# Expert places of 64, 96, 64, 96, 96, 64, 96, 64 slots with the first expert in one of 64, and the norm's weight row moved from routing to the gathered rows

## The chip, the core and the metric

The kernel runs on one core of a Trainium2 chip. The metric is the device time of one execution in microseconds, the median of the runs. Of the core's engines the text speaks of TensorE (PE, matrix products; its weight loads are PEld), VectorE (DVE), ScalarE (ACT), GpSimd (POOL) and SyncE (SP), which here does little but issue the transfers that bring weights from HBM. Everything is in float32.

## The reference

A two-layer decoder trunk over 256 tokens of width 1024. Layer 0 has two kinds of attention and a dense SwiGLU, layer 1 a sliding-window attention beside a short convolution and then a top-2-of-8 expert SwiGLU, which is where the change lies:

```python
def moe_swiglu(x, w_router, w_gate, w_up, w_down):      # x = rms_norm(h, norm_ffn)
    xt = x.reshape(B * S, D)                            # 256 x 1024
    logits = (xt @ w_router).astype(jnp.float32)        # 256 x 8
    top_vals, top_idx = lax.top_k(logits, TOP_K)        # 2 of 8
    top_w = jax.nn.softmax(top_vals, axis=-1)
    gates = jnp.einsum('nk,nke->ne', top_w, jax.nn.one_hot(top_idx, N_EXPERTS, ...))
    for e in range(N_EXPERTS):
        y = y + gates[:, e:e + 1] * swiglu(xt, w_gate[e], w_up[e], w_down[e])
def rms_norm(x, g):
    return x * rsqrt(mean(x * x) + eps) * g
```

`swiglu(x) = (silu(x @ w_gate) * (x @ w_up)) @ w_down` with an inner width of 3584, so one expert has 3 x 1024 x 3584 float32 weights, 44 MB, and the eight have 352 MB.

## The kernel before

**The stages.** Layer 0 and the attention of layer 1 run to about 490 us. Then the router chooses (`route1` to `route3`, `logits`, `choose`), and from about 506 us the eight experts run one after the other (`experts`, `L1085`) to the end.

**Places and slots.** An expert works on a fixed number of slots, not on all 256 tokens. `CAPS` (`L32`) gives eight places of 96 or 64 slots. Place 0 always holds expert 0, whose weights can so be loaded before the routing is known; the other seven experts are sorted by how many tokens chose them, and `RANKS` (`L33`) says which of them stands in place 1, 2, ... (rank 0 has most tokens). The weights' addresses of places 1 to 7 are read from `most` into SP's registers (`read_counts`). Should an expert have more tokens than its place has slots, a branch behind everything (`L1317`) runs a further pass for it (`rest`) with that expert's weights loaded again.

**Gather.** `dispatch` makes a 0/1 matrix of tokens by slots on DVE, `gather` multiplies it with the normalised rows `xg` on PE, so that a place's tokens stand side by side, and DVE and ACT copy the product from PSUM to `g`. Places are gathered in groups, `((0,), (1, 2), (3, 4), (5, 6), (7,))`: the first before any expert runs, each other one between the steps of the expert ahead of it.

**Steps and weights.** An expert has 12 steps, each on one transfer of 3584 KB (3.67 MB): two of `gate`, two of `up`, for each half `r` of the inner width, and four of `down`. `into` (`L1140`, matmuls at `L1150`) does a gate or up step: 4 x 4 matmuls for each 32 slots, so 32 for a place of 64 and 48 for one of 96. `down` (`L1186`) does 28 matmuls of 512 columns into `y` (`L1193`), and for a place of 96 another 28 of 256 columns into `yo` (`L1197`). `weights.send()` at the end of each step issues the next transfer of a list into a ring of five buffers `big`, so a transfer's issue on SP (`L1124` for gate and up, `L1132` for down) waits until the step five transfers ahead of it has let its buffer go. Between the steps `put` sets the small work (`fill`): transposes of the hidden rows (`act_T`), the gather of the next group, and the weighted sum of the previous expert's result into `h` (`part_y`, `scatter`).

**The start of the ring.** Two of the five buffers exist since layer 0 and are filled there with expert 0's two first gate transfers. The pool of the other three is opened in `experts_open` (`L1019`) where `np`, `xp` and `parts` lay before; the three transfers that it sends at once (up, up, gate) wait until the last readers of that memory are done. `parts` holds the split weights of the dense layers, three pairs of tiles in one pool.

**Routing.** `route2` (`L898`) squares `h` on ACT for the norm and multiplies `h` by the norm's weight row `gain` on DVE into `xf`; `route3` (`L902`) makes the reciprocal root on POOL and scales `xf` by it into `xg` on ACT. The row itself is a transfer that POOL issues in `route_open`. `final_gain` (`L1280`) is another one, of the weights of the very last norm, into one of the tiles `t.dr`. The router itself works on `h` with the weight row folded into its own matrix (`conv_w`, `L809`).

Of the kernel before, what the change touches and what calls it, by code (L numbers as in the profile page):

```python
# [18 lines left out]
D = 1024  # L19
KD = D // 128  # L20
S = 256
NB = 2
# [6 lines left out]
BIG = 7168  # L29
NPARTS = 3  # L30

CAPS = (96, 64, 96, 64, 96, 64, 96, 64)  # L32
RANKS = (3, 0, 4, 1, 5, 2, 6)  # L33

# [54 lines left out]
def trunk(ctx: ExitStack, tc: tile.TileContext, a: dict, out: bass.AP):  # L89
# [14 lines left out]
    raw_pools = []  # L104
    partss = ExitStack()
    parts = rpool(partss, "parts", NPARTS)
    pre = ExitStack()
    xp = rpool(pre, "xp")
    prec = ExitStack()
    pc_ = rpool(prec, "prec")  # L110
# [40 lines left out]
    def split(u):  # L151
        if u.load.view is None:
            load(u.load)
        v, n, w = u.load.view[:, u.j0:u.j0 + u.n], u.n, u.load.at[4]
        pool, size = parts, 2048
        hi, lo = (pool.tile([128, size], F32R, name=x)[:, :n * w].rearrange("p (k w) -> p k w", k=n)
                  for x in ("whi", "wlo"))
        A.activation(hi, v, AF.Copy)  # L158
        m = w - w // u.pool // 2 * 2 if w >= 256 else w
        V.tensor_tensor(lo[:, :, :m], v[:, :, :m], hi[:, :, :m].bitcast(F32), op=OP.subtract)  # L160
        if m < w:
            G.tensor_tensor(lo[:, :, m:], v[:, :, m:], hi[:, :, m:].bitcast(F32), op=OP.subtract)  # L162
        u.hl = (hi, lo)

    ahead_max = [0]

# [94 lines left out]
    def load_gain(name, eng):  # L261
        t.gain = row(a[name], D, "gain", t.np, eng)
# [54 lines left out]
    place = consts.tile([128, 2, NE], F32, name="place")  # L317
    wr = consts.tile([128, KD, NE], F32, name="wr")
    cs = pc_.tile([128, 2, NB, 48], F32, name="cs")

# [483 lines left out]
    def conv_w():  # L804
# [3 lines left out]
        T.transpose(pcw[:, 1, 0:8], t.g8, ident[:8, :8])  # L808
        V.tensor_tensor(wr, wr, pcw[:, 1, 0:8][:, :, None].to_broadcast([128, KD, NE]), op=OP.mult)  # L809

# [58 lines left out]
    def route_open():  # L869
# [6 lines left out]
        t.hT, t.ww, t.sq = {}, wide(), bank()  # L876
        open_("np", "rt")
        t.xf = t.np.tile([128, NB, D], F32, name="xf")
        load_gain('l1_norm_ffn', G)

# [3 lines left out]
    def route1(b, i):  # L884
        xfT = t.np.tile([128, 4, 128], F32, name="xfT", bufs=2)
        p = tbank()
# [11 lines left out]
    def route2(b, i):  # L898
        A.activation(t.sq, h[:, b, half[i]], AF.Square, scale=1.0 / math.sqrt(D), accum_out=t.rs[:, b, i:i + 1])
        V.tensor_tensor(t.xf[:, b, half[i]], h[:, b, half[i]], t.gain[:, half[i]], op=OP.mult)  # L900

    def route3(b):  # L902
        r = t.rs[:, b]
        V.tensor_scalar(r[:, 2:3], r[:, 0:1], r[:, 1:2], EPS, op0=OP.add, op1=OP.add)
        G.tensor_tensor(r[:, 3:4], r[:, 2:3], nhalf, op=OP.pow)
        A.activation(t.xg[:, b], t.xf[:, b], AF.Copy, scale=r[:, 3:4])

# [111 lines left out]
    def experts_open():  # L1019
        close("np")  # L1020
        pre.close()
        partss.close()
        pws.close()
# [7 lines left out]
        for _ in range(3):  # L1031
            weights.send()
        t.dr = [draw[0].tile([128, RAW], F32, name="raw") for _ in range(2)]
        t.ep = rpool(ctx, "ep", 2)
# [50 lines left out]
    def experts(base, caps, groups, first=(), then=(), finish=()):  # L1085
# [11 lines left out]
        def gather(g, k0):  # L1097
# [6 lines left out]
            for s in g:  # L1104
                if s not in gath:
                    gath[s] = t.ep.tile([128, KD, NG * O], F32, name="g", bufs=3)
                o, v = gath[s][:, k0:k0 + 2, :caps[s]], p[:, :, group[s][1]:group[s][1] + caps[s]]
                if k0 // 2 % 2:
                    V.tensor_copy(o, v)  # L1109
                else:  # L1110
                    A.activation(o, v, AF.Copy)

# [183 lines left out]
    def final3(b):  # L1296
# [4 lines left out]
    finish = [do(final_in)] + [do(final2, b) for b in range(NB)] + [do(final3, b) for b in range(NB)]  # L1301
    mine = experts((0,) * NE, CAPS, ((0,), (1, 2), (3, 4), (5, 6), (7,)), [do(experts_open)],
                   [do(order.close), do(in_order, 'PE'), do(arrange), do(gates), do(read_counts)], finish)
# [52 lines left out]
```

## Time and profile before

| | us |
|---|---|
| median of 3 runs | 1349.49 (1349.46 to 1352.29) |
| the profiled execution | 1352.92 |
| its span, first to last instruction | 1351.1 |
| PE busy | 1287.5 (95%) |
| DVE, ACT, POOL busy | 377.6 (28%), 297.6 (22%), 167.7 (12%) |
| moved by DMA | 432 MB, 320 GB/s over the span |

The page gives each engine's busy time, then the span in 40 equal slices of 33.8 us with busy tenths, then the chain of work that ended last. PE's 95% says little by itself: it is a mean over layers, where the weights are split by three engines, and experts, where PE multiplies what the DMA brings. The chain of the page goes to 76% over PE and to 15% over DMA, nearly all of that on the experts' weights.

### The profile page before, as it was taken

To read this page: it belongs to the slowest core of one execution; us is meant where nothing else is said; L and a number is where in the kernel's file an instruction comes from. 1 tells how busy PE (TensorE), PEld (TensorE's weight loads), DVE (VectorE), ACT (ScalarE), POOL (GpSimd) and SP (SyncE) were. 2 spreads that over 40 slices of the span, in tenths; PEclk is the share of its full clock that TensorE was granted. 3 is DMA by queue.
4 is the path that set the end of the run, shared out by engine and by line. 5 is a ranking of instruction groups with operands and counts; after the bars stand their busy time and mean duration, and the time that the engine had idled before them with its cause. 6 is when DMAs were issued, how large, how long until landed. Compare 5 with 4: busy or idle time off the path is not lost.

```text
span 1351.1 us, 23865 instructions
## 1 busy us (share of the span) xinstructions
PE 1287.5 (95%) x10713; PEld 696.8 (52%) x10713; DVE 377.6 (28%) x704; ACT 297.6 (22%) x471; POOL 167.7 (12%) x117
## 2 busy tenths in 40 slices
PE   7999899999999999999999999989999989999985
PEld 6876678888879773433332343322343323343332
DVE  7666444455465840001100100100100200101202
ACT  6555444333344620101000101001000001000001
POOL 3311344344434110000000000000000000000000
PEclk9998899999999999999999999999999999999997
DMA  8620784555555369989999999999999999999992
GB/s 269 204 93 1 276 297 164 195 176 185 186 168 176 114 244 378 371 342 421 420 429 412 425 430 411 424 426 416 424 426 413 426 421 419 425 419 420 425 421 105
DMA packets 75903, 432.24 MB, mean 320 GB/s; under 512 B 3692, under 2 KB 7808, under 8 KB 71568
## 3 DMA queue, kind: packets, MB, share of 16 engines
q1 hardware_dynamic: 75088, 428.48, 79.6%
q8 instruction: 86, 1.41, 0.4%
q0 software_dynamic: 560, 1.62, 0.4%
q10 hardware_dynamic: 144, 0.52, 0.1%
q14 instruction: 25, 0.20, 0.0%
HBM read 429.57 MB, written 1.05 MB: 319 GB/s over the span
## 4 chain that ended last, share of the span: by engine, by line
PE 76%; DMA 15%; DVE 2%; ACT 1%; POOL 1%; issue 0%; SPq 0%; POOLq 0%; ACTq 0%
PE mm L1150 30%; DMA big<-in_l_w_up_dram 12%; PE y L1193 9%; PE mm L199 8%; PE mm L200 8%; PE mm L201 7%; PE yo L1197 4%; DMA big<-in_l_w_down_dram 2%; PE tt L1102 2%; PE ww L370 1%; PE tt L1177 1%; PE ww L199 1%; PE ww L200 1%; PE ww L201 1%; DMA raw<-in_l_w_gate_dram 1%; PE mm L413 1%
## 5 line engine op out<-in xcount | busy, mean ns | idle before, releaser
L1150 PE MATMUL mm<-big,g 128*32 128x448 f32 x5120 | 497.5, 546 | 20.6 <-DMA big<-in_l_w_up_dram 14.3
L1150 PEld LDWEIGHTS mm<-big,g 128*32 128x32 f32 x5120 | 165.8, 111 | 330.9 <-issue 308.3
L1193 PE MATMUL y<-big,ehT 128*32 128x512 f32 x1792 | 214.7, 593 | 0.5 <-DMA big<-in_l_w_down_dram 0.5
L162 POOL TENSOR_TENSOR wlo<-raw,whi 128x288 fp32r<-128x288 f32 (+6 forms) x74 | 154.5, 2088 | 287.2 <-ACT whi L158 267.0
L160 DVE TENSOR_TENSOR wlo<-raw,whi 128x1760 fp32r<-128x1760 f32 (+6 forms) x74 | 142.9, 1932 | 134.3 <-ACT whi L158 133.9
L158 ACT ACTIVATE whi<-raw 128x2048 fp32r<-128x2048 f32 (+4 forms) x74 | 134.5, 1817 | 154.5 <-PE mm L201 75.2
L199 PE MATMUL mm<-whi,xh 128*128 128x512 f32 (+3 forms) x352 | 138.3, 393 | 1.9 <-ACT whi L158 1.1
L200 PE MATMUL mm<-wlo,xh 128*128 128x512 f32 (+3 forms) x352 | 136.7, 388 | 3.0 <-POOL wlo L162 3.0
L201 PE MATMUL mm<-whi,xl 128*128 128x512 f32 (+3 forms) x352 | 136.7, 389 | 2.4 <-DVE xl L288 2.4
L1178 ACT ACTIVATE ehT<-tt 128x512 f32<-128x512 f32 (+1 forms) x32 | 15.6, 487 | 474.5 <-PE tt L1177 474.4
L1294 POOL TENSOR_TENSOR fs<-fs,nhalf 128x1 f32<-128x1 f32 x2 | 1.1, 548 | 844.1 <-DVE fs L1293 844.1
L1193 PEld LDWEIGHTS y<-big,ehT 128*32 128x32 f32 x1792 | 57.1, 110 | 84.0 <-issue 63.7
L1164 DVE TENSOR_TENSOR hid<-hid,mm 128x448 f32<-128x448 f32 x40 | 24.9, 622 | 264.9 <-PE mm L1150 261.8
L199 PEld LDWEIGHTS mm<-whi,xh 128*128 128x128 f32 x352 | 67.3, 191 | 17.5 <-ACT xh L287 1.7
L201 PEld LDWEIGHTS mm<-whi,xl 128*128 128x128 f32 x352 | 67.2, 191 | 17.6 <-DVE xl L288 4.1
L200 PEld LDWEIGHTS mm<-wlo,xh 128*128 128x128 f32 x352 | 67.3, 191 | 16.9 <-POOL wlo L162 3.3
L1197 PE MATMUL yo<-big,ehT 128*32 128x256 f32 x896 | 68.9, 379 | 0.0
L1197 PEld LDWEIGHTS yo<-big,ehT 128*32 128x32 f32 x896 | 29.1, 110 | 67.0 <-issue 66.6
L1109 DVE COPY g<-tt 128x192 f32<-128x192 f32 (+1 forms) x16 | 4.6, 321 | 162.0 <-PE tt L1102 162.0
L199 PE MATMUL mm<-xh,whi 128*128 128x256 f32 x160 | 46.5, 291 | 0.0
L200 PE MATMUL mm<-xl,whi 128*128 128x256 f32 x160 | 45.3, 283 | 0.0
L201 PE MATMUL mm<-xh,wlo 128*128 128x256 f32 x160 | 45.2, 283 | 0.0
(311 smaller groups left out, 1051.9 us busy)
## 6 DMA issues: line engine op xcount, KB each, us to landing
big<-in_l_w_up_dram SPq DMA_DIRECT2D x32, 3584.0 KB, 26.6
big<-in_l_w_down_dram SPq DMA_DIRECT2D x31, 3584.0 KB, 24.7
big<-in_l_w_gate_dram SPq DMA_DIRECT2D x30, 3584.0 KB, 25.7
raw<-in_l_w_in_dram SPq DMA_DIRECT2D x15, 1024.0 KB, 5.1
raw<-in_l_w_gate_dram SPq DMA_DIRECT2D x14, 1024.0 KB, 5.2
raw<-in_l_w_up_dram SPq DMA_DIRECT2D x14, 1024.0 KB, 5.2
raw<-in_l_w_down_dram SPq DMA_DIRECT2D x14, 1024.0 KB, 5.0
raw<-in_l_w_out_dram SPq DMA_DIRECT2D x8, 1024.0 KB, 5.2
```

Of the source, the lines that this page charges most:

```text
L158: A.activation(hi, v, AF.Copy)
L160: V.tensor_tensor(lo[:, :, :m], v[:, :, :m], hi[:, :, :m].bitcast(F32), op=OP.subtract)
L162: G.tensor_tensor(lo[:, :, m:], v[:, :, m:], hi[:, :, m:].bitcast(F32), op=OP.subtract)
L199: T.matmul(ps, l[0], r[0], start=first, stop=False, **kw)
L200: T.matmul(ps, l[0], r[1], start=False, stop=False, **kw)
L201: T.matmul(ps, l[1], r[0], start=False, stop=last, **kw)
L1102: T.matmul(p[:, k], t.xg[:, b, (k0 + k) * 128:(k0 + k + 1) * 128], d[g][:, b, :n], start=(b == 0), stop=(b == 1))
L1150: T.matmul(ps[key][j][i * O:(i + 1) * O], x[:, k0 + k, g * O:(g + 1) * O], w[:, k, c:c + CH], **at)
L1164: V.tensor_tensor(x[:, g], x[:, g], ps["u"][g], op=OP.mult)
L1178: copy = V.tensor_copy if j0 else lambda a_, b_: A.activation(a_, b_, AF.Copy)
L1193: T.matmul(t.y[c * O:(c + 1) * O], x[:, (2 * i + c % 2) * O:(2 * i + c % 2 + 1) * O], w[:, j, c // 2 * 512:(c // 2 + 1) * 512], **at)
L1197: T.matmul(t.yo[c * O:(c + 1) * O], x[:, (4 + i) * O:(5 + i) * O], w[:, j, c * 256:(c + 1) * 256], **at)
```

## The change

It does four things.

- **Slots.** `CAPS` becomes (64, 96, 64, 96, 96, 64, 96, 64): four places of each kind as before, expert 0 in one of 64, and places 3 and 4 of 96 side by side. `RANKS` puts the four experts with most tokens in the places of 96. The groups of the gather become (0), (1, 2), (3), (4, 5), (6, 7).
- **The norm's weight row.** `xf`, its four multiplications and the row's transfer are gone; `xg` is `h` times the reciprocal root. The weights, kept as a column for each of the eight 128-wide pieces (`gk`), are applied when the gathered product is copied out of PSUM: on DVE as a multiplication with `gk` spread over the slots, on ACT as a copy with the column as its scale, one instruction for each of the two pieces.
- **Which engine copies.** A group of one place is copied by ACT alone; in groups of two every other product goes to DVE, as before.
- **Memory.** `parts` becomes three pools of one pair of tiles each, taken in turn, and stands behind `xp`; the router's transposes go into one of the tiles `t.dr`, which are taken earlier.

```diff
-CAPS = (96, 64, 96, 64, 96, 64, 96, 64)
-RANKS = (3, 0, 4, 1, 5, 2, 6)
+CAPS = (64, 96, 64, 96, 96, 64, 96, 64)
+RANKS = (0, 4, 1, 2, 5, 3, 6)
...
-    parts = rpool(partss, "parts", NPARTS)
...
+    parts = [rpool(partss, f"parts{i}") for i in range(NPARTS)]
...
-        pool, size = parts, 2048
+        pool, size = parts[(LAST - part[0]) % NPARTS], 2048
+        part[0] += 1
...
-        V.tensor_tensor(wr, wr, pcw[:, 1, 0:8][:, :, None].to_broadcast([128, KD, NE]), op=OP.mult)
+        V.tensor_copy(gk, pcw[:, 1, 0:8])
+        V.tensor_tensor(wr, wr, gk[:, :, None].to_broadcast([128, KD, NE]), op=OP.mult)
...
-        open_("np", "rt")
-        t.xf = t.np.tile([128, NB, D], F32, name="xf")
-        load_gain('l1_norm_ffn', G)
+        t.dr = [draw[0].tile([128, RAW], F32, name="raw") for _ in range(2)]
...
-        xfT = t.np.tile([128, 4, 128], F32, name="xfT", bufs=2)
+        xfT = t.dr[0][:, (2 * b + i) * 512:(2 * b + i + 1) * 512].rearrange("p (k c) -> p k c", k=4)
...
-        V.tensor_tensor(t.xf[:, b, half[i]], h[:, b, half[i]], t.gain[:, half[i]], op=OP.mult)
...
-        A.activation(t.xg[:, b], t.xf[:, b], AF.Copy, scale=r[:, 3:4])
+        A.activation(t.xg[:, b], h[:, b], AF.Copy, scale=r[:, 3:4])
...
-                if k0 // 2 % 2:
-                    V.tensor_copy(o, v)
-                else:
-                    A.activation(o, v, AF.Copy)
+                if k0 // 2 % 2 and len(g) > 1:
+                    V.tensor_tensor(o, v, gk[:, k0:k0 + 2, None].to_broadcast([128, 2, caps[s]]), op=OP.mult)
+                    continue
+                for k in range(2):
+                    A.activation(o[:, k], v[:, k], AF.Copy, scale=gk[:, k0 + k:k0 + k + 1])
...
-    mine = experts((0,) * NE, CAPS, ((0,), (1, 2), (3, 4), (5, 6), (7,)), [do(experts_open)],
+    mine = experts((0,) * NE, CAPS, ((0,), (1, 2), (3,), (4, 5), (6, 7)), [do(experts_open)],
```

What it moves is seen at three places. Up to the routing every engine has the same instructions in the same order as before.

On SP, from the last transfer of the dense weights to the first that a step of expert 0 releases, with the semaphores that each waits for; before:

```order
L148 DMA raw<-in_l_w_out_dram 128x4x512 [waits DMAHW1_49,DVE_49,Pool_49]
L1124 DMA big<-in_l_w_up_dram 128x4x1792 [waits DVE_49,DMASW1_49,PE_49,Activation_49]
L1124 DMA big<-in_l_w_up_dram 128x4x1792 [waits DVE_49,PE_49,Pool_49]
L1124 DMA big<-in_l_w_gate_dram 128x4x1792 [waits DMASW5_49,PE_49,Activation_49]
L1037 TENSOR_LOAD most [waits DVE_49]
L1037 ISA x2
L1124 DMA big<-in_l_w_gate_dram 128x4x1792 [waits PE_49]
```

and after:

```order
L149 DMA raw<-in_l_w_out_dram 128x4x512 [waits DMAHW1_49,DVE_49,Pool_49]
L1124 DMA big<-in_l_w_up_dram 128x4x1792 [waits DVE_49,DMASW1_49,PE_49,Activation_49]
L1124 DMA big<-in_l_w_up_dram 128x4x1792 [waits DVE_49,PE_49,Pool_49]
L1124 DMA big<-in_l_w_gate_dram 128x4x1792
L1036 TENSOR_LOAD most [waits DVE_49]
L1036 ISA x2
L1124 DMA big<-in_l_w_gate_dram 128x4x1792 [waits PE_49]
```

The third transfer into the new buffers no longer waits for the routing (the weight row, the logits, `xg`); the first two wait for the same instructions as before, and the fourth for the end of expert 0's first step.

On POOL, from the last splits of dense weights (`wlo`) over the two reciprocal roots of the routing (`rs`) to those of the last norm (`fs`); before:

```order
L162 TENSOR_TENSOR wlo<-raw,whi 128x4x72 x8
L128 DMA gain<-in_l_norm_ffn_dram 128x1024
L162 TENSOR_TENSOR wlo<-raw,whi 128x4x72
L1283 DMA raw<-in_final_norm_dram 128x1024
L162 TENSOR_TENSOR wlo<-raw,whi 128x4x72
L905 TENSOR_TENSOR rs<-rs,nhalf 128x1 x2
L1294 TENSOR_TENSOR fs<-fs,nhalf 128x1 x2
```

and after:

```order
L164 TENSOR_TENSOR wlo<-raw,whi 128x4x72 x10
L906 TENSOR_TENSOR rs<-rs,nhalf 128x1
L1283 DMA raw<-in_final_norm_dram 128x1024
L906 TENSOR_TENSOR rs<-rs,nhalf 128x1
L1294 TENSOR_TENSOR fs<-fs,nhalf 128x1 x2
```

The weight row's transfer is gone, and the transfer for the last norm stands between the two reciprocal roots of the routing, where it waits for the last logits, whose transposes lie in the tile that it fills.

On PE, the start of expert 0, from its gather (`L1102`, after `L1101`) on; before:

```order
L1102 MATMUL tt<-disp,xg 128x96 x16
L1037 TENSOR_LOAD most
L1150 MATMUL mm<-big,g 32x448 x48
L1118 MATMUL tt<-ident,disp 96x128 x2
L1150 MATMUL mm<-big,g 32x448 x192
L1177 MATMUL tt<-ident,hid 128x128 x7
L1177 MATMUL tt<-ident,hid 64x128 x7
L1150 MATMUL mm<-big,g 32x448 x48
L1102 MATMUL tt<-disp,xg 128x160 x4
```

and after:

```order
L1101 MATMUL tt<-disp,xg 128x64 x16
L1036 TENSOR_LOAD most
L1150 MATMUL mm<-big,g 32x448 x32
L1118 MATMUL tt<-ident,disp 64x128 x2
L1150 MATMUL mm<-big,g 32x448 x128
L1177 MATMUL tt<-ident,hid 128x128 x7
L1150 MATMUL mm<-big,g 32x448 x32
L1101 MATMUL tt<-disp,xg 128x160 x8
L1193 MATMUL y<-big,ehT 32x512 x28
```

Each step of expert 0 has two thirds of its matmuls, and its down steps have none into `yo`; the gather of the next group stands where it stood.

## Rows read from the trace of the kernel before

**Rows 1.** The page: 40 slices of 33.8 us, DMA busy tenths and GB/s.

```profile
DMA  8620784555555369989999999999999999999992
GB/s 269 204 93 1 276 297 164 195 176 185 186 168 176 114 244 378 371 342 421 420 429 412 425 430 411 424 426 416 424 426 413 426 421 419 425 419 420 425 421 105
```

**Rows 2.** Busy time by stretch; the last columns are granted clock, DMA share, GB/s.

```profile
500.00:620.00 120.00, 118.06 (x1231) 48.67 (x1234) 13.68 (x66) 9.91 (x23) 0.00 (x0) 1.00 0.94 372
640.00:1300.00 660.00, 640.08 (x6481) 237.74 (x6477) 70.24 (x131) 48.26 (x98) 0.00 (x0) 0.99 1.01 422
```

**Rows 3.** The page: transfers by line; KB of one, median us from issue to landing.

```profile
big<-in_l_w_up_dram SPq DMA_DIRECT2D x32, 3584.0 KB, 26.6
...
raw<-in_final_norm_dram POOLq DMA_DIRECT2D x1, 512.0 KB, 5.5
```

**Rows 4.** Timeline of SP: start, duration, engine, line; issues of expert 0 and 1.

```profile
494.95 0.37 SPq L1124 DMA_DIRECT2D big<-in_l_w_up_dram  x1
499.71 0.37 SPq L1124 DMA_DIRECT2D big<-in_l_w_gate_dram  x1
515.01 0.37 SPq L1124 DMA_DIRECT2D big<-in_l_w_gate_dram  x1
524.53 0.34 SPq L1132 DMA_DIRECT2D big<-in_l_w_down_dram  x1
...
604.90 0.40 SPq L1124 DMA_DIRECT2D big<-in_l_w_up_dram  x1
610.91 0.39 SPq L1124 DMA_DIRECT2D big<-in_l_w_up_dram  x1
```

**Rows 5.** Waits of SP, 465 to 620 us: total us, times, longest.

```profile
SPq L1124 <- PE mm L1150: 49.5, 6, 10.6
```

**Rows 6.** Timeline of PE: steps of a place of 96, of 64, last steps.

```profile
505.74 9.23 PE L1150 MATMUL mm<-big,g 128*32 128x448 f32 x96 [1.04 <-DVE gate L1016]
...
594.33 1.35 PE L1102 MATMUL tt<-disp,xg 128*128 128x160 f32 x8
...
611.84 6.22 PE L1150 MATMUL mm<-big,g 128*32 128x448 f32 x64
...
1313.06 6.22 PE L1150 MATMUL mm<-big,g 128*32 128x448 f32 x64 [2.39 <-DMA big<-in_l_w_up_dram]
...
1321.68 12.22 PE L1193 MATMUL y<-big,ehT 128*32 128x512 f32 x112 [0.46 <-DMA big<-in_l_w_down_dram]
```

**Rows 7.** Timeline of POOL in the routing.

```profile
471.02 0.58 POOL L1283 DMA_DIRECT2D raw<-in_final_norm_dram  x1 [0.30 <-POOL wlo L162]
...
497.95 0.55 POOL L905 TENSOR_TENSOR rs<-rs,nhalf 128x1 f32<-128x1 f32 x1 [5.74 <-DVE rs L904]
```

**Rows 8.** Timeline of ACT, end of routing, first copy of the gather.

```profile
498.53 1.15 ACT L906 ACTIVATE xg<-xf,rs 128x1024 f32<-128x1024 f32 x1 [0.91 <-POOL rs L905]
502.11 0.33 ACT L1111 ACTIVATE g<-tt 128x192 f32<-128x192 f32 x1 [2.43 <-PE tt L1102]
```

**Rows 9.** Timeline of DVE: the weight row, gather copy, and registers' source `most`.

```profile
495.65 0.69 DVE L900 TENSOR_TENSOR xf<-h,gain 128x512 f32<-128x512 f32 x1
...
504.73 0.36 DVE L1109 COPY g<-tt 128x192 f32<-128x192 f32 x1 [0.23 <-PE tt L1102]
505.01 0.14 DVE L981 TENSOR_SCALAR most<-ei 128x1 int32<-128x1 f32 x1
```

**Rows 10.** Timeline of SP: issues that steps of place 2 (96 slots) release.

```profile
744.74 0.38 SPq L1124 DMA_DIRECT2D big<-in_l_w_up_dram  x1
...
810.09 0.38 SPq L1124 DMA_DIRECT2D big<-in_l_w_up_dram  x1
...
823.31 0.37 SPq L1124 DMA_DIRECT2D big<-in_l_w_gate_dram  x1
843.36 0.35 SPq L1132 DMA_DIRECT2D big<-in_l_w_down_dram  x1
```

**Rows 11.** A stretch of 2 us just after PE waited for weights.

```profile
726.00:728.00 2.00, 2.00 (x16) 0.65 (x12) 0.00 (x0) 0.00 (x0) 0.00 (x0) 0.50 1.02 423
```

More of the change, by code (lines that the diff above doesn't have):

```diff
@@ L30 @@
 NPARTS = 3
-CAPS = (96, 64, 96, 64, 96, 64, 96, 64)
-RANKS = (3, 0, 4, 1, 5, 2, 6)
+LAST = 1
+CAPS = (64, 96, 64, 96, 96, 64, 96, 64)
+RANKS = (0, 4, 1, 2, 5, 3, 6)
 def _pieces(x, bits, n):
@@ L104, in trunk @@
     raw_pools = []
-    partss = ExitStack()
-    parts = rpool(partss, "parts", NPARTS)
     pre = ExitStack()
     xp = rpool(pre, "xp")
+    partss = ExitStack()
+    parts = [rpool(partss, f"parts{i}") for i in range(NPARTS)]
     prec = ExitStack()
@@ L163, in split @@
         u.hl = (hi, lo)
-    ahead_max = [0]
+    ahead_max, part = [0], [0]
     def limit(n):
@@ L318, in trunk @@
     wr = consts.tile([128, KD, NE], F32, name="wr")
+    gk = consts.tile([128, KD], F32, name="gk")
     cs = pc_.tile([128, 2, NB, 48], F32, name="cs")
@@ L1019, in experts_open @@
     def experts_open():
-        close("np")
+        partss.close()
         pre.close()
-        partss.close()
         pws.close()
@@ L1032, in experts_open @@
             weights.send()
-        t.dr = [draw[0].tile([128, RAW], F32, name="raw") for _ in range(2)]
         t.ep = rpool(ctx, "ep", 2)
```

## The prediction

> **What bounds the kernel now.** I read the slices of the page first, because the means of the page mix layers and experts. From slice 19 (608 us) to the last but one the DMA row stands at 9 and the rate at 410 to 430 GB/s: there the transfers of the experts' weights run without a gap. In slices 16 to 18, the first expert, the rate is only 378, 371 and 342 GB/s, though the transfers are of the same kind [rows 1]. [...] PE is busy for 118 of 120 us in the first stretch, so there it is PE that holds the DMA up, and later the other way round. The waits of SP say how: between 465 and 620 us it waited longest for steps of expert 0 (`L1150`) to give a buffer back [rows 5].
>
> The sizes fit that. A transfer has 3584 KB [rows 3], 3.67 MB, so 8.7 us at 422 GB/s. A gate or up step of a place of 96 takes PE 9.0 us and one of 64 takes 6.0 us (9.23 and 6.22 with the tail of the last matmul [rows 6]). Expert 0, with 96 slots, is slower per buffer than the DMA, and it starts with the ring nearly full, so it never gets through the ring: every transfer waits for it. The later 64-slot places win that back, and at the end PE waits for weights: 2.39 us before an up step and 0.46 before the last two down steps [rows 6]. So the end of the run is set by when the last weights land, and that by how long the DMA stood idle since its stream began at 494.95 us. What lies behind (the last steps, the sums, the final norm) is the same before and after, as the last place has 64 slots in both.
>
> **The change part by part.**
>
> *Expert 0 in 64 slots.* Its first step starts at 505.74 us [rows 6]. With 64 slots the steps end at about 511.9, 518, 524, ... where before the releases came at 515.01, 524.53 and so on to 604.90 [rows 4]. The transfers issued at 494.95 and directly behind it keep the DMA busy for 2 x 8.7 us, to about 512.4, plus the one or two microseconds that an issue needs to move data; the first release comes before that has run out, and from there a release every 6 to 9 us meets a transfer of 8.7. So the DMA should have no gap in expert 0. The gain by bytes: (422 - 372) GB/s x 120 us = 6.0 MB, which is 14.2 us. By issues: twelve transfers were issued from 494.95 to 604.90; without gaps the twelfth would end 12 x 8.7 = 104.4 us after 494.95, before it ended 8.7 after 604.90, a difference of 14.2. The DMA share gives less: 0.94 against 1.01 [rows 2] is 8.3 us of 120. [...]
>
> *The third transfer no longer waits for the routing.* It was issued at 499.71 [rows 4] behind one that was under way until about 505, so issuing it at 495.3 gains **nothing** by itself.
>
> *The transfer of the last norm's weights moves.* It has 512 KB [rows 3], 1.2 us of all sixteen engines at 422 GB/s. POOL issued it at 471.02 [rows 7], in time for a gap of the stream (slice 15 has 244 GB/s [rows 1]); now it comes behind the last logits, at about 498.2, into the stream. Cost between 0, if it fits into gaps between packets, and 1.2; a share of 1.01 leaves no gaps, so I take **1.2 us on**. The row itself says nothing of sharing. [...]
>
> *What is queued behind it on POOL.* The second reciprocal root ran at 497.95 for 0.55 us [rows 7] and `xg` followed at 498.53 for 1.15 [rows 8]. Now the root stands behind a transfer that starts at about 498.2 and holds POOL for 0.58, so `xg` ends at about 500.5 instead of 499.68. The gather is the one that waits for it, and it started at 500.9, because the 0/1 matrix from DVE comes then. Covered; without the cover it would be 0.9 us, and even that would come out of the slack of the next point.
>
> *The weight row at the gather.* Four multiplications of 0.69 us go from DVE [rows 9]; they ran beside PE's last dense matmuls. Two copies of `g` of 0.36 go too, and these stood in DVE's chain to `most`, which PE reads into a register before the first step: `most` was done at 505.15 and the step started 0.6 us later (the profile puts that wait down to the DVE instruction that had just ended [rows 6]; the order has PE read `most` there). So the first step should start 0.5 to 1 us sooner. ACT gets eight copies of 128x64 with a column as scale for two of 128x192 at 0.33 [rows 8]; at no more than 0.33 each that is 2.6 us from about 501.5, done before the step starts. In later groups ACT has two to four short copies where it had one or two, while it is idle most of the time. All of this lies ahead of a release that is not on the path any more: **0**, within 1 us either way.
>
> *Places 3 and 4, both of 96.* This is the price of the new order. With places alternating, PE falls behind in one and recovers in the next. From place 2: six steps with the gather of the next group took 65.35 us (744.74 to 810.09) against 52.2 of DMA, the last two down steps 20.05 (823.31 to 843.36) against 17.4 [rows 10], and its first four, at 9.0 to 9.3, about 37 against 34.8. So PE falls back by some 13.2 + 2.6 + 2.3 = 18 us in a place of 96. Two in a row give 36, less 5.4 because place 4 has no gather of four times 1.35 [rows 6], less 5.4 for the two short down steps of place 2 that fall into place 3, less 2.6 for those of place 4 that fall into place 5: 22 us. The ring lets PE be four transfers behind, 34.8 us, of which a step that has just caught up uses 9.0 and the issue about 2: some 24. So the DMA just doesn't run dry. [...] I take **1 us on**, between 0 and 10.
>
> *The rest.* `gk` adds a copy of 128x8 on DVE; `parts` in three pools leaves order and waits of the dense layers as they are: 0.
>
> **Sum:** -13.5 + 1.2 + 1 = -11.3 us. The profiled execution took 1352.92 us, so 1341.6; the median of the runs lies 3.4 us below that execution, which makes the forecast **1338.2 us**.
>
> **The rivals.**
>
> *The pair of 96 gives the gain back.* If none of the deductions above holds, the two places put PE 36 us behind where 26 are allowed, and the DMA idles for 10 us late instead of 14 early: 1338.2 + 9 = 1347. For it: 22 against 24 is a thin margin. Against it: each deduction is a step that stands in the order. Time 1342 to 1347.
>
> *No change.* The lower rate in expert 0 might not come from releases but from the memory itself, or something else in that stretch; then faster releases only queue transfers longer. For it: a DMA share of 0.94, nearly full. Against it: SP's waits name PE, and 422 GB/s is reached with the same transfers. It gives 1349 to 1351. [...]
>
> *Slower: expert 0 has more than 64 tokens.* Then the branch at the end runs a second pass for it: twelve more transfers, 12 x 8.7 = 104 us, with a first landing and last steps of some 25 us that nothing covers: about 1470 us. It decides at 65 tokens. The router of the reference, on its inputs, gives expert 0 58 tokens and the others 72, 69, 65, 64, 62, 61 and 61: the four largest go to 96 slots and the rest fit 64.
>
> **How the numbers follow.** Forecast 0.70 (its own range 1335 to 1342, from 8.3 to 14.2 gained and 0 to 3 lost at the pair); the pair 0.14; no change 0.09; the further pass 0.02; something not seen here 0.05, mostly on the slow side. The range runs from 1334.5, a little below the full 14.2 with the transfer for nothing, to 1345, which takes in most of the pair's cases. A measurement of this kernel tells about 0.2%, 2.7 us, from no change. Faster by more: 0.70, most of the pair's 0.14 and a little of the rest, 0.85; within: 0.10; slower: 0.05.
>
> **What would show it.** In the profile of the changed kernel the rate from 500 to 620 us should be 415 GB/s or more, and SP should issue the twelfth transfer before 590 us. PE should wait for weights already at place 0 or 1. The first step should start at 504.7 to 505.7. Around places 3 and 4, some 900 to 1030 us, the rate should hold 410 or more; a slice of 380 there would be the pair's price. The stretch from the last landing to the end should be as long as before. The prediction is wrong if the rate of the first stretch rises and the end doesn't move, or if the rate doesn't rise.

## The result, and the profile after

The changed kernel takes 1338.53 us (median of 6 runs, 1335.82 to 1342.88) where the kernel before takes 1350.45 beside it: a ratio of 0.9907, 95% interval 0.9892 to 0.9922, so 10.5 to 14.6 us faster. The forecast was 1338.2. The total was right, and that it came so close is luck: two of its terms were wrong, and they cancel. The places 3 and 4 cost some six times what was put down for them, and about as much came back from something that the forecast had costed at nothing, 32 bytes in SBUF. The profiled execution took 1339.13 us with a span of 1337.3. One later execution of the changed kernel, at a granted clock of 0.557, took 2190 us and is left out of every figure below.

The page of the changed kernel, DMA and rate in 40 slices of 33.4 us, to be held against [rows 1]:

```profile
DMA  8620785555555249999999999999999999999993
GB/s 272 207 93 1 294 287 189 182 177 178 187 166 181 95 183 433 415 427 431 422 426 430 416 428 425 424 432 386 397 384 399 429 420 428 434 419 426 427 426 134
```

The dip of slices 16 to 18 is gone, and a new one stands in slices 28 to 31, 902 to 1036 us: 384 to 399 GB/s. The table by stretches (columns as in [rows 2]; last granted clock, DMA share, GB/s) says it closer, with three slices out of the new dip:

```profile
500.00:620.00 120.00, 119.75 (x1192) 46.03 (x1194) 10.59 (x52) 13.30 (x33) 0.00 (x0) 1.00 1.01 425
640.00:880.00 240.00, 230.29 (x2361) 87.92 (x2353) 22.32 (x44) 20.85 (x49) 0.00 (x0) 0.99 1.01 424
900.00:1020.00 120.00, 119.10 (x1294) 44.97 (x1290) 12.12 (x22) 8.24 (x17) 0.00 (x0) 1.00 0.97 388
1040.00:1280.00 240.00, 238.87 (x2445) 89.30 (x2441) 28.62 (x51) 20.43 (x43) 0.00 (x0) 0.99 1.01 426
...
960.00:980.00 20.00, 20.00 (x210) 7.68 (x206) 1.26 (x3) 1.98 (x5) 0.00 (x0) 1.00 0.92 354
980.00:1000.00 20.00, 20.00 (x252) 7.94 (x248) 0.00 (x0) 0.79 (x2) 0.00 (x0) 1.00 0.99 392
1000.00:1020.00 20.00, 20.00 (x220) 6.92 (x216) 1.86 (x3) 0.00 (x0) 0.00 (x0) 1.00 0.95 382
```

The first stretch went from 372 to 425 GB/s. From 640 to 880 us, where the DMA is full in both kernels, the rate is 424 with the change and 422 without [rows 2]; from 1040 to 1280 us it is 426. That looks like nothing and is one of the two surprises.

SP's issues: the second of the three transfers that `experts_open` sends into the new buffers, and the twelfth counted from it (before 494.95 and 604.90, [rows 4]). With the second the unbroken stream begins; the first had gone out by itself at 469.39 us (before at 471.51). Then the two issues on which the working for places 3 and 4 rests:

```profile
493.80 0.37 SPq L1124 DMA_DIRECT2D big<-in_l_w_up_dram  x1
...
571.55 0.40 SPq L1124 DMA_DIRECT2D big<-in_l_w_up_dram  x1
...
824.05 0.35 SPq L1132 DMA_DIRECT2D big<-in_l_w_down_dram  x1
...
1015.17 0.38 SPq L1124 DMA_DIRECT2D big<-in_l_w_up_dram  x1
```

PE: the first step of expert 0; the first step that waited for weights; place 3's first gate step and its two up steps, before which it waited for the last time ahead of the new dip; and the last two down steps (before 505.74 and 1321.68, [rows 6]):

```profile
504.13 6.22 PE L1150 MATMUL mm<-big,g 128*32 128x448 f32 x64 [0.20 <-issue]
...
760.21 6.22 PE L1150 MATMUL mm<-big,g 128*32 128x448 f32 x64 [1.34 <-DMA big<-in_l_w_up_dram]
...
777.70 9.23 PE L1150 MATMUL mm<-big,g 128*32 128x448 f32 x96 [0.86 <-DMA big<-in_l_w_gate_dram]
...
813.06 19.94 PE L1150 MATMUL mm<-big,g 128*32 128x448 f32 x192 [3.41 <-DMA big<-in_l_w_up_dram]
...
1308.12 12.22 PE L1193 MATMUL y<-big,ehT 128*32 128x512 f32 x112 [0.42 <-DMA big<-in_l_w_down_dram]
```

**A yardstick.** The span is not the best measure of a single profile here: the second transfer into the new buffers was issued between 490.9 and 499.6 us in the profiles below, also in kernels that are the same up to there. So I give for each profiled kernel the *stretch*, from that issue to the start of the last two down steps. It is 1321.68 - 494.95 = 826.7 us before and 1308.12 - 493.80 = 814.3 after: 12.4 less. The remaining 1.4 of the 13.8 us between the spans are 1.15 of an earlier start and 0.2 in the tail. It is one execution each, and it holds the last up step, which took 6.22 us in these two, in the places alone and in the kernel before, moved, but 7.7 to 7.9 in the other profiles that end on a place of 64. Differences of one or two us between stretches therefore say little.

### The profile page after: what moved, and what is told of

Same layout as the page of the kernel before. It is cut to its first block, busy times and chain, and to the rows that moved or that the text cites. A ratio compares the mean times of both kernels' runs of the same rounds, so it can differ in the third digit from the quotient of the medians.

```text
span 1337.3 us, 23873 instructions
## 1 busy us (share of the span) xinstructions
PE 1285.7 (96%) x10713; PEld 697.2 (52%) x10713; DVE 373.7 (28%) x697; ACT 303.3 (23%) x495; POOL 167.3 (13%) x116
## 4 chain that ended last, share of the span: by engine, by line
PE 82%; DMA 11%; DVE 2%; ACT 1%; POOL 1%; issue 0%; POOLq 0%; ACTq 0%
PE mm L1150 32%; PE y L1193 11%; PE mm L201 8%; PE mm L202 8%; PE mm L203 8%; DMA big<-in_l_w_up_dram 8%; PE yo L1197 4%; DMA big<-in_l_w_down_dram 2%; PE tt L1177 1%; PE tt L1101 1%; PE ww L373 1%; PE ww L203 1%; PE ww L201 1%; PE ww L202 1%; PE mm L416 1%; DMA raw<-in_l_w_gate_dram 1%
## 5 line engine op out<-in xcount | busy, mean ns | idle before, releaser
L1150 PE MATMUL mm<-big,g 128*32 128x448 f32 x5120 | 495.1, 544 | 11.6 <-DMA big<-in_l_w_up_dram 10.5
L201 PEld LDWEIGHTS mm<-whi,xh 128*128 128x128 f32 x352 | 67.7, 192 | 17.6 <-issue 1.8
L1180 DVE COPY ehT<-tt 128x384 f32<-128x384 f32 x16 | 8.9, 558 | 124.0 <-PE tt L1177 124.0
```

The lines of the kernel that those rows point to most:

```text
L201: T.matmul(ps, l[0], r[0], start=first, stop=False, **kw)
L1150: T.matmul(ps[key][j][i * O:(i + 1) * O], x[:, k0 + k, g * O:(g + 1) * O], w[:, k, c:c + CH], **at)
```

## The experiments

Times are given as difference to the kernel before by the ratio to its runs beside it, with the 95% interval. The runs came in three groups, each on a chip of its own: the two halves, three places of 96 and all places of 64 (median of the kernel before 1351.48); the kernel before moved, the change not moved, the change again and three places of 96 in a row (1351.08); the rest (1350.29).

### One half of the change each

The places alone; the kernel before with

```diff
-CAPS = (96, 64, 96, 64, 96, 64, 96, 64)
-RANKS = (3, 0, 4, 1, 5, 2, 6)
+CAPS = (64, 96, 64, 96, 96, 64, 96, 64)
+RANKS = (0, 4, 1, 2, 5, 3, 6)
...
-    mine = experts((0,) * NE, CAPS, ((0,), (1, 2), (3, 4), (5, 6), (7,)), [do(experts_open)],
+    mine = experts((0,) * NE, CAPS, ((0,), (1, 2), (3,), (4, 5), (6, 7)), [do(experts_open)],
```

> The kernel before with only the places changed (64, 96, 64, 96, 96, 64, 96, 64, their ranks and the groups of the gather); the weight row, the memory and the copies stay as before. Theory: the gain of 11.9 us comes from expert 0 in 64 slots, which lets the DMA run without a gap, so this kernel should be faster than the one before by 10 to 13 us, and 500 to 620 us should show 415 GB/s or more. The first step should start later than in the full change, by 0.5 to 1 us, without the end moving for it. Rival: the earlier start of the stream (third transfer without the routing) or of the first step is needed for the gain; then this kernel gains less than 8 us and the rate of the first stretch stays under 405 GB/s.

The other half: the changed kernel with these three lines taken back.

> The changed kernel with the places, ranks and groups of the kernel before, so only the weight row, the memory and the copies are changed. Theory: nothing of this lies ahead of what sets the end, so the time is within 0 to 1.5 us of the kernel before (the last norm's transfer may cost 1.2), and 500 to 620 us shows about 372 GB/s again. Rival: an earlier first step counts while PE bounds expert 0; since each buffer of expert 0 comes back that much sooner, the time would fall by 1 to 3 us.

The places alone gave -9.9 us (-12.2 to -7.7), just short of the 10 to 13 expected, stretch 816.6. The rest alone gave **-7.7 us** (-10.1 to -5.3), stretch 820.6, where 0 to +1.5 was expected, and more than its rival had, too. Together that would be -17.6, and the change has -12.6. The stretches of the two, places alone first:

```profile
500.00:620.00 120.00, 118.26 (x1162) 45.48 (x1166) 11.12 (x55) 10.79 (x23) 0.00 (x0) 0.99 1.00 416
...
640.00:880.00 240.00, 231.11 (x2385) 87.63 (x2381) 23.02 (x46) 18.23 (x39) 0.00 (x0) 0.99 1.01 421
```

and the rest alone:

```profile
500.00:620.00 120.00, 119.15 (x1251) 47.19 (x1253) 10.26 (x41) 12.64 (x32) 0.00 (x0) 1.00 0.96 381
...
640.00:880.00 240.00, 237.28 (x2395) 87.69 (x2389) 26.34 (x49) 18.08 (x39) 0.00 (x0) 0.99 1.01 424
1040.00:1280.00 240.00, 233.85 (x2397) 87.57 (x2391) 27.93 (x49) 19.67 (x41) 0.00 (x0) 0.99 1.01 426
```

The places do what was said of them: 416 GB/s in the first stretch, and a first step that comes 1.1 us later than in the change, counted from the same issue. The rest leaves that stretch nearly as it was (381), but where the DMA is full it runs at 424 to 426 instead of 421 to 422. Over the 800 us of the stream 0.8% is 6.4 us, about what this half gained (7.7 by the times, 6.1 by the stretches). Nothing in this half moves fewer bytes in the experts. But `gk`, a constant tile of 128x8 float32, takes 32 bytes of each partition, and the buffers `big` lie behind the constants. In the built programs all five of them stand 32 bytes higher after the change: 27136, 55808, 111712, 140384 and 169056 instead of 27104, 55776, 111680, 140352 and 169024. So there was a new theory to test.

### The 32 bytes

The kernel before, moved; and the full change, not moved:

```diff
-    slot = consts.tile([128, 128], F32, name="slot")
+    slot = consts.tile([128, 136], F32, name="slot")
```

```diff
-    slot = consts.tile([128, 128], F32, name="slot")
+    slot = consts.tile([128, 120], F32, name="slot")
```

(with the iota that fills `slot` over as many columns; no more than 96 are read).

> The kernel before with one constant tile (slot) 32 bytes longer per partition, so all five weight buffers lie 32 bytes higher in SBUF, at the very addresses of the changed kernel (27136, 55808, 111712, 140384, 169056 for 27104, 55776, 111680, 140352, 169024); no instruction is added and nothing else is changed. New theory, formed because the rest of the change alone gained 8 us and its stream ran at 424 to 426 GB/s for 422: the rate depends on where the buffers lie, and the column gk moved them. Then this kernel shows 424 to 426 GB/s from 640 to 880 us and is 5 to 7 us faster than the kernel before. Rival: the rate comes from the copies or the memory of the routing; then 422 GB/s and no gain, within 1.5 us.

> The full change, but the constant tile slot is 32 bytes shorter, which makes room for gk, so the weight buffers lie where they lay before; everything else is the full change. Theory of the addresses: 421 to 422 GB/s from 640 to 880 us, and the time 5 to 7 us above the full change of the same call, near 1344. Rival (copies, memory of the routing): 424 to 426 GB/s and the time of the full change.

> The full change once more, unaltered, on the chip of the other kernels of this call, as their yardstick. 10 to 14 us faster than the kernel before, 424 to 426 GB/s from 640 to 880 us, and 354 to 411 GB/s in the slices of 20 us from 900 to 1020 us.

The kernel before, moved, took -5.1 us (-7.4 to -2.7), stretch 821.1. The change, not moved, took -7.8 (-10.9 to -4.9), stretch 818.4. The change itself, taken again beside them, took -11.5 (-15.1 to -7.8); no rates are read from its profile. In the built programs the tiles that PE and ACT use all through the experts (`g`, `disp`, `hid`, `ehT`) stay where they were; with the five buffers move the constants behind `slot`, the tiles `raw`, `xg` and the small tiles of the routing. The kernel before, moved:

```profile
640.00:880.00 240.00, 236.78 (x2409) 87.72 (x2405) 26.33 (x49) 17.11 (x35) 0.00 (x0) 1.00 1.01 424
1040.00:1280.00 240.00, 232.43 (x2377) 86.75 (x2373) 28.51 (x51) 18.14 (x35) 0.00 (x0) 0.99 1.01 422
```

The change, not moved:

```profile
640.00:880.00 240.00, 228.92 (x2365) 87.20 (x2361) 22.32 (x44) 20.85 (x49) 0.00 (x0) 0.99 1.01 421
1040.00:1280.00 240.00, 238.87 (x2457) 89.33 (x2453) 28.62 (x51) 20.43 (x43) 0.00 (x0) 1.00 1.01 422
```

Both point to the addresses, with one blemish: the moved kernel's second stretch is back at 422 (it was at 427 and 425 from 1240 on, and at 407 and 399 in the two slices of 20 us before that, which no other kernel has; without those two the stretch has 426, and what they are stays open). And in the change the effect is smaller than the 5 to 7 us expected, 3.7 by the times, whose intervals overlap, and 4.1 by the stretches. So it was tried again where no pair of 96 is in the way.

### Without the pair, at three addresses

```diff
-CAPS = (64, 96, 64, 96, 96, 64, 96, 64)
-RANKS = (0, 4, 1, 2, 5, 3, 6)
+CAPS = (64, 96, 64, 96, 64, 96, 64, 64)
+RANKS = (0, 3, 1, 4, 2, 5, 6)
```

(with the groups of the kernel before). The fourth of the seven sorted experts has 64 tokens in these inputs, so three places of 96 hold them all.

> The changed kernel with places of 64, 96, 64, 96, 64, 96, 64, 64 slots: expert 0 in 64, no two places of 96 side by side, one place of 96 fewer (the fourth largest expert has 64 tokens and fits). Theory: the pair of 96 is what lowered the rate to 354 to 411 GB/s from 900 to 1020 us; here no stretch after 640 us should fall below 410, and the time should be 0 to 3 us below that of the full change. If every GB/s missing there is paid at the end, it is (424 - 388) GB/s x 120 us = 4.3 MB, 10 us, and the time should be 8 to 10 us below the full change, near 1329.

The same with `slot` 32 bytes shorter, so that the buffers lie as before:

> Three places of 96, with the tile slot 32 bytes shorter, so that the weight buffers lie where they lay in the kernel before. Nothing else differs from the run with three places of 96. Theory of the addresses: 421 to 422 GB/s and 5 to 7 us more than that run, so 13 to 15 us below the kernel before; here no pair of 96 takes a part of the effect back. Rival: no effect without the pair; then 425 GB/s and about 20 us below the kernel before.

And the same with the three upper buffers moved on to multiples of 512 bytes:

```diff
-        t.rs = t.rp.tile([128, NB, 4], F32, name="rs")
+        t.rs = t.rp.tile([128, NB, 56], F32, name="rs")
```

> Three places of 96 (64, 96, 64, 96, 64, 96, 64, 64) as before, with one tile of the routing (rs) 416 bytes longer, so that the three upper weight buffers start at 112128, 140800 and 169472, multiples of 512 as the two lower ones (27136, 55808). Nothing else differs from the run with three places of 96, in which the upper ones lay 96 bytes past a multiple. Theory of the addresses: buffers at multiples of 512 are filled fastest, so the rate from 640 to 880 us rises from 425 to 427 to 430 GB/s, and the time falls by another 3 to 7 us, to 24 to 27 us below the kernel before. Rival: only the move away from the old addresses matters; then 425 GB/s and about 20 us below the kernel before.

They took -13.6 us (-15.9 to -11.5) at the old addresses, **-20.1** (-23.0 to -17.4) at those of the change, and **-23.9** (-26.5 to -21.3) at multiples of 512. At the old addresses:

```profile
640.00:880.00 240.00, 230.28 (x2389) 85.94 (x2385) 22.43 (x44) 18.34 (x41) 0.00 (x0) 0.99 1.01 420
900.00:1020.00 120.00, 112.50 (x1117) 41.84 (x1109) 12.00 (x26) 10.57 (x25) 0.00 (x0) 0.99 1.01 420
1040.00:1280.00 240.00, 216.08 (x2156) 79.68 (x2145) 24.87 (x43) 17.42 (x38) 0.00 (x0) 0.99 1.01 422
```

At those of the change:

```profile
640.00:880.00 240.00, 231.52 (x2401) 86.62 (x2397) 22.43 (x44) 18.34 (x41) 0.00 (x0) 0.99 1.01 425
900.00:1020.00 120.00, 115.09 (x1137) 42.56 (x1129) 12.00 (x26) 11.14 (x26) 0.00 (x0) 0.99 1.01 425
1040.00:1280.00 240.00, 219.78 (x2174) 80.87 (x2169) 24.87 (x43) 17.43 (x38) 0.00 (x0) 0.98 1.01 426
```

At multiples of 512:

```profile
640.00:880.00 240.00, 231.36 (x2420) 86.74 (x2416) 22.41 (x44) 18.32 (x41) 0.00 (x0) 1.00 1.01 427
900.00:1020.00 120.00, 113.41 (x1125) 41.61 (x1128) 13.26 (x28) 12.43 (x29) 0.00 (x0) 0.99 1.01 427
1040.00:1280.00 240.00, 218.46 (x2181) 79.43 (x2177) 20.18 (x36) 17.39 (x38) 0.00 (x0) 0.98 1.01 427
```

420 to 422, 425 to 426, 427: with a DMA share of 1.01 in all nine rows, and between the first and second nothing changed but the place of the buffers and of the few tiles that move with them; between the second and third only the three upper buffers and the small tiles of the routing. The stretches go along: 815.1, 808.4 and 804.0 us. The second was taken on another chip than the first and third, but the two other kernels taken on their chip with buffers at the addresses of the change (the last place of 96 and the eight more transfers, below) show 424 to 427 GB/s in the same stretches. The address is therefore shown as the cause: 10.3 us between the first and third, side by side, of which the first 32 bytes are 6.5 by the times (6.7 by the stretches). The further 3.8 (4.4), at the low end of the 3 to 7 expected, rest on the rates and stretches, as the intervals of those two times overlap. The last of the three is the fastest kernel of this study, 1327.17 us. It holds only as long as the fourth expert has no more than 64 tokens.

Why addresses matter, no run here shows. At the old addresses two of the buffers start 480 bytes past a multiple of 512 and three 64 past; at those of the change two start at one and three 96 past; in the last run all five start at one. The mean of the two long stretches rises by 1.1% from the first to the second and by 1.4% from the first to the last, from 421 to 427. Which buffers gained, and from which multiple on, was not taken apart.

### The price of the pair

The run with three places of 96 at the addresses of the change also has no dip: 425 GB/s from 900 to 1020 us where the change has 388. Its expectation left two sizes open, 0 to 3 us or 8 to 10. It came out between: 7.5 us by the times (-20.1 against -12.6), 5.9 by the stretches. This run also has one place of 96 fewer, but three of them together are worth no more than 1.8 to 3.1 us once no pair is in the way (the run with none, below). The dose was raised as well:

```diff
-CAPS = (64, 96, 64, 96, 96, 64, 96, 64)
-RANKS = (0, 4, 1, 2, 5, 3, 6)
+CAPS = (64, 64, 96, 96, 96, 64, 96, 64)
+RANKS = (4, 0, 1, 2, 5, 3, 6)
```

> The full change with places of 64, 64, 96, 96, 96, 64, 96, 64 slots: three places of 96 side by side, the same number of places of each kind. Theory: PE falls back by some 18 us in a place of 96, the ring allows some 24 in all, so the third place in a row costs what it falls back, less what is not yet used up: 12 to 18 us on top of the full change, with slices of 20 us at 330 to 390 GB/s in the third place. Rival: the DMA engines are not level with each other when they idle, so that a mean rate that falls costs little at the end, as one reading of the full change had it; then 0 to 4 us on top.

It took +2.6 us (+0.4 to +4.7), slower than the kernel before, and 14 to 15 slower than the change (stretch 828.7, 14.4 more), as expected. The rate falls from the second of its places of 96 on (first row) and furthest in the third (second row):

```profile
900.00:920.00 20.00, 20.00 (x212) 7.46 (x208) 2.42 (x5) 0.00 (x0) 0.00 (x0) 1.00 0.86 347
...
980.00:1000.00 20.00, 20.00 (x210) 7.71 (x206) 1.26 (x3) 2.23 (x6) 0.00 (x0) 1.00 0.87 325
```

PE is busy for all of both slices: PE sets the pace there and the DMA idles, as the theory has it. A third place of 96 in a row costs 14 to 15 us, a second one 6 to 8, since the ring pays for the rest of that.

The other way to avoid neighbours, with four places of 96:

```diff
+CAPS = (64, 96, 64, 96, 64, 96, 64, 96)
+RANKS = (0, 4, 1, 5, 2, 6, 3)
```

(with the groups of the kernel before).

> The full change with places of 64, 96, 64, 96, 64, 96, 64, 96 slots: four of each kind, no two of 96 side by side, and the last one of 96. Theory: the price of the pair (some 4 to 8 us) is gone, but PE falls back by some 18 us in the last place and nothing behind it hides that, so the stretch from the last landing to the end grows by 13 to 18 us, and the kernel is 6 to 13 us slower than the full change, 0 to 6 us below the kernel before. Rival: PE catches up in the last place too, as its waits for weights at the end suggest; then it is 4 to 8 us faster than the full change.

It took -4.5 us (-6.2 to -2.6), 8 worse than the change, in the lower half of what was expected. The stream ended sooner than in the change, but PE was behind. Stretches of the end:

```profile
1300.00:1310.00 10.00, 9.62 (x102) 4.24 (x98) 3.12 (x6) 1.35 (x3) 0.00 (x0) 1.00 0.29 121
1310.00:1320.00 10.00, 10.00 (x128) 3.93 (x124) 0.00 (x0) 0.00 (x0) 0.00 (x0) 1.00 0.01 2
```

and its last down matmuls:

```profile
1326.23 0.61 PE L1197 MATMUL yo<-big,ehT 128*32 128x256 f32 x8
```

The weights were there before 1310 us and the steps ended at 1326.8; in the change the stream ends after 1310 and the steps at 1320.3. So a pair in the middle is the cheaper place for the fourth 96.

### What PE's work is worth

```diff
+CAPS = (64,) * 8
+RANKS = (0, 1, 2, 3, 4, 5, 6)
```

(with the groups of the kernel before, and the count for the branch set to 96, so that this kernel leaves out the tokens beyond 64 of its largest experts).

> The changed kernel with all eight places of 64 slots and the count for the branch taken against 96, so the tokens beyond 64 of the three largest experts (8, 5 and 1) are left out; PE loses about 37 us of steps in each of the four places of 96. Theory: the landing of the weights sets the end, so about 148 us less work on PE change the time by no more than the pair's price: 0 to 4 us below the full change, the rate 415 GB/s or more all through, and PE waits for weights at nearly every step. Rival: PE, at 96% of the span, still bounds the experts at several places; then the time falls by 15 us or more.

It took -21.9 us (-24.1 to -19.9), stretch 805.3: 3.1 less than with three places of 96, by the times 1.8, which is within the intervals. Against the change it is 9.3 less, where 0 to 4 was expected: the pair's price had been put too low, as just seen. PE's busy time fell by 105 us against the change (1285.7 to 1180.3). What became of it stands in its waits from 500 to 1330 us (total us, times, longest):

```profile
PE mm L1150 <- DMA big<-in_l_w_up_dram: 48.5, 28, 2.5
PE y L1193 <- DMA big<-in_l_w_down_dram: 45.2, 23, 2.5
PE mm L1150 <- DMA big<-in_l_w_gate_dram: 20.5, 12, 2.9
```

114 us of waiting for weights, where the change has 11.8. Once no pair is in the way the stream alone sets the end.

### What a transfer beside the stream costs

Three places of 96 at the addresses of the change, and in `final_gain`

```diff
-        G.dma_start(t.gfin, bass.AP(tensor=g.tensor, offset=g.offset, ap=[[0, 128], [1, D]]))
+        for _ in range(9):
+            G.dma_start(t.gfin, bass.AP(tensor=g.tensor, offset=g.offset, ap=[[0, 128], [1, D]]))
```

> Three places of 96, and the transfer of the last norm's 512 KB made nine times in place of once, all on POOL behind the second reciprocal root, each into the same tile. Theory: a transfer of POOL shares the sixteen engines with the weights, so eight more cost 8 x 1.2 = 9.9 us when the stream has no gap: about 10 us below the kernel before. Rival: they fit into gaps; then 0 to 2 us and 18 to 20 us below the kernel before.

It took -9.2 us (-12.3 to -6.1), 10.9 more than without the eight; the stretch is 818.1, 9.7 more than 808.4. Two of the nine on POOL, and the last down steps:

```profile
498.13 0.64 POOL L1284 DMA_DIRECT2D raw<-in_final_norm_dram  x1 [6.45 <-PE mm L897]
...
576.45 0.53 POOL L1284 DMA_DIRECT2D raw<-in_final_norm_dram  x1 [7.79 <-DMA raw<-in_final_norm_dram]
```

```profile
1312.48 12.22 PE L1193 MATMUL y<-big,ehT 128*32 128x512 f32 x112 [0.32 <-ACT ehT L1178]
```

They were over by 590 us, and the end some 730 us later is still late by their bytes: 9.7 / 8 = 1.2 us each. Nothing behind gives that back.

## Why the prediction was right, and where it was not

Two of the runs without the pair and the change itself make a path from the kernel before in three steps, and so a second sum beside the one of the forecast (stretches; times in brackets). The first step takes several edits together and has one place of 96 fewer, which the third gives back:

| term | forecast | measured |
|---|---|---|
| expert 0 in 64, routing, the last norm's transfer | -13.5 + 1.2 + 0 | -11.6 (-13.6): three of 96 at the old addresses |
| `gk` moves the buffers by 32 bytes | 0 | -6.7 (-6.5): the same at the new addresses |
| places 3 and 4 both of 96 | +1 | +5.9 (+7.5): the change against that |
| sum | -11.3 | -12.4 (-12.6) |

**What bounds the kernel.** Right. Taking 105 us of work from PE is worth 9.3 us, most of it the pair's price; eight transfers early in the stream cost their full time at the end, 9.7 us.

**Expert 0 in 64 slots, -13.5.** Right, as far as the runs separate it: 372 to 425 GB/s in the first stretch, the twelfth transfer issued at 571.55 instead of 604.90, and -12.8 if the last norm's 1.2 is taken out of the -11.6. Counting bytes, which gives 14.2, was nearer than the DMA share's 8.3. No run shows the 13.5 itself, which lies between these two counts; what the runs show in its place is the -12.8.

**The last norm's transfer, +1.2.** Right, by the run with eight more: 9.7 us by the stretches, 1.2 each.

**What is queued behind it on POOL; the weight row at the gather.** Half right. The rows of POOL and ACT in the changed kernel:

```profile
497.52 0.63 POOL L1283 DMA_DIRECT2D raw<-in_final_norm_dram  x1 [6.47 <-PE mm L897]
498.17 0.59 POOL L906 TENSOR_TENSOR rs<-rs,nhalf 128x1 f32<-128x1 f32 x1
```

```profile
498.79 1.15 ACT L907 ACTIVATE xg<-h,rs 128x1024 f32<-128x1024 f32 x1 [2.38 <-POOL rs L906]
501.35 0.52 ACT L1111 ACTIVATE g<-tt,gk 128x64 f32<-128x64 f32 x2 [1.41 <-PE tt L1101]
```

The root stands behind the transfer, as said, and `xg` comes 5.0 us after the first issue instead of 3.6 [rows 4, 8]. It was not quite covered: PE's gather started at 500.13, right behind `xg`, 6.3 us after that issue where it was 5.95. The first step nevertheless came 10.3 us after it for 10.8 before, at the small end of the half to one us, with copies on ACT of 0.26 us each. All of this is worth no more than was put down, 0, or 1.2 with the last norm's transfer: the rest of the change, without the 32 bytes, is -0.5 us by the stretches on the old places (820.6 against 821.1) and +1.8 on the new ones (818.4 against 816.6), by the times -2.6 and +2.1, all within what single profiles and the intervals leave open.

**`gk`, "0".** This step failed, and it is the one that the text passed over in half a sentence. `gk` was costed as an instruction, a copy of 128x8. It is also a tile, and what lies behind it in SBUF moves, the five buffers among it. The forecast looked at what the change executes and not at where it puts things; no row of the trace shows addresses, so only building both kernels and comparing them would have told.

**Places 3 and 4, +1.** The mechanism was right, the size was not, though its range of 0 to 10 held it. The forecast let PE fall back by 22 us of 24 allowed. One of its deductions was empty: "5.4 for the two short down steps of place 2 that fall into place 3". They stand between place 3's gate steps and its up steps, and PE waited 3.41 us for weights before those up steps, at 813.06. Up to there it was level with the DMA, and short steps only made it wait. From that wait on the count starts anew: SP issued 20 transfers from 824.05 to 1015.17, 19 intervals in 191.1 us, while at 8.7 us each they would have taken 165.3. PE fell back by 25.8 us; with the empty deduction taken out, and the first four steps of place 3 with their 2.3 us, which lie before the wait, the forecast's own sum is 22 + 5.4 - 2.3 = 25.1. That is 1 to 2 us over the 24. The forecast's 1 us no run shows by itself. What the runs show in its place is, on top of the 25.8, a slower step at a fallen clock: behind the wait at 813.06 the granted clock was 0.60 and 0.55.

```profile
814.00:816.00 2.00, 2.00 (x19) 0.56 (x12) 0.00 (x0) 0.00 (x0) 0.00 (x0) 0.60 1.04 431
816.00:818.00 2.00, 2.00 (x16) 0.59 (x12) 0.00 (x0) 0.00 (x0) 0.00 (x0) 0.55 1.00 409
```

The two up steps took 19.94 us, two such steps of place 1 at 603.05, without a wait, 18.48. These 1.5 us lie in the first of them, which ends before 824.05, so they are not in the 25.8. Together that is some 3 of the 6 us; the rest is open. The ring may allow less than was taken, which no run shows. Of what was taken off for it, the 2 us of an issue fit the trace of before: with the transfer issued at 494.95 the rate is 0 to 14 GB/s up to 496.0, 143 to 272 up to 497.5 and 430 in the half microsecond behind that. (The forecast isn't at one with itself on what the ring allows either: 24 us in the sum, 26 in the rival of the pair.)

**The two errors may not be independent.** With the pair the 32 bytes are worth 3.7 us by the times and 4.1 by the stretches, without it 6.5 and 6.7. The intervals are too wide to show that these differ; a reading that fits is that while PE sets the pace, as from 960 to 980 us with PE busy for 20.00 us and a DMA share of 0.92, a faster DMA only idles more.

**What would show it.** Of the six signs three held: the rate of the first stretch, the twelfth transfer and the stretch behind the last landing. The first step started at 504.13, ahead of the 504.7 to 505.7 named, since the stream itself began 1.15 us sooner. PE did not wait for weights at place 0 or 1 but first at 760.21, in place 2: in expert 0 the DMA ran full while PE was still working off the ring. The third failure is the one that told: "some 900 to 1030 us, the rate should hold 410 or more". It was 388 on the mean of 900 to 1020 us. With the end where the forecast had it, that alone says that something else must have paid. The price of the pair is not 10 us, as its missing bytes would have it ((424 - 388) GB/s x 120 us = 4.3 MB); why it is less, no run shows. The last section has how the stream ends with a hold-up and without.

## What to carry to other kernels

A total that comes out right confirms no term of it; only runs that make one edit at a time do, and the sign that fails in a trace is worth more than the time that fits. A new tile, even one of 32 bytes, can move every buffer that lies behind it, and where a kernel lives on its transfers the start addresses belong to the cost of an edit and are worth a try by themselves (here 10 us from the old ones to multiples of 512 bytes). When a lag is added up over several steps, begin at the last wait of the engine that lags, since time gained before it is gone.

## What the runs showed of the hardware

**Start addresses of the buffers.** Transfers of the same bytes ran at 420 to 422 GB/s, at 425 to 426 and at 427, by where in SBUF their buffers start, see above.

**How the stream ends.** The end of the stream in slices of 5 us, with three places of 96, whose stream never had a gap:

```profile
1295.00:1300.00 5.00, 5.00 (x48) 1.61 (x44) 0.00 (x0) 0.00 (x0) 0.00 (x0) 0.85 0.67 283
1300.00:1305.00 5.00, 3.87 (x35) 1.61 (x31) 1.80 (x3) 0.60 (x1) 0.00 (x0) 1.00 0.48 203
1305.00:1310.00 5.00, 5.00 (x52) 1.56 (x48) 0.00 (x0) 0.00 (x0) 0.00 (x0) 1.00 0.31 128
```

and in the changed kernel, where PE had held it up at 900 to 1020 us:

```profile
1305.00:1310.00 5.00, 3.77 (x36) 1.75 (x31) 1.80 (x3) 0.60 (x1) 0.00 (x0) 1.00 0.94 399
1310.00:1315.00 5.00, 5.00 (x52) 1.75 (x45) 0.00 (x0) 0.00 (x0) 0.00 (x0) 1.00 0.44 184
1315.00:1320.00 5.00, 5.00 (x52) 1.71 (x44) 0.00 (x0) 0.00 (x0) 0.00 (x0) 1.00 0.01 5
```

Without a gap the DMA share falls to a half and a third for some 15 us before the last byte is there; after a hold-up it does so for 5. The other profiles go the same way, if not by as much: with a hold-up at 900 to 1020 us (the places alone, the change not moved, three places in a row) two slices of 5 us lie between 0.1 and 0.9, without one (three places of 96 at the old addresses, eight more transfers) three, but at multiples of 512 and with all places of 64 also two. Why, no run shows: the profile gives the mean of the DMA engines and doesn't list them one by one.
